# Layer-norm beta by accumulating transfers, gamma on VectorE and rstd on ScalarE or VectorE, and the last w2 tile pair by plain products, in an eight-core encoder kernel

## The chip, the cores and the metric

The kernel runs on all eight cores of one Trainium2 chip (two dies of four cores), one sequence of the batch on each core, without traffic between cores. The metric is the device time of the slowest core in microseconds (us).

A program on all eight cores has two states on this chip. In the slow one, the cores of one die or of both are granted a lower TensorE clock and take some per cent longer. Each run therefore carries a state, and only fast runs enter a verdict. I also give the **undisturbed cores**: over all runs of a kernel, the median span of the cores whose granted clock was within 0.012 of the ninth decile of that kernel's clocks. It leaves out the wait for the slowest core, so it is some 5 to 10 us below a fast run's time, but it is steady. I compare it only with the kernel before on the same chip.

## The reference

Two post-norm layers over x of shape (8, 2048, 1024) in float32. Each layer is a token mixer and a dense MLP, and each of these is followed by a layer norm, so there are four norms:

```python
x = layer_norm(alpha * x + mix, ln_g[i, 0], ln_b[i, 0])
x = layer_norm(alpha * x + squared_relu_mlp(x, mlp_w1[i], mlp_w2[i]), ln_g[i, 1], ln_b[i, 1])

def layer_norm(x, g, b):          # cut
    y = (xf - mu) * lax.rsqrt(var + LN_EPS) * g + b
```

Mixer 0 is a gated MLP with 128-position blocks, mixer 1 a short gated convolution. The MLP has 4096 hidden units. beta (`b` above, `ln_b`) is one row of 1024 numbers for each norm, the same for all positions.

## The kernel before

A Python scheduler lays out all operations. Each operation states what it reads and writes and for how long it is thought to run; a list scheduler gives each engine its order, and semaphores are added for the dependences. Each engine runs its own queue in order. A paced transfer gets a wait for the oldest transfers still out until no more than 1.6 MB are out:

```python
DMA_WINDOW = 1.6e6
DMA_RATE = 290e3                  # bytes per us that the model takes for every transfer
...
if op.is_dma:
    while op.paced and low < len(issued) and total - issued[low][0] > DMA_WINDOW:
        op.deps.setdefault(issued[low][1].idx, True)     # wait for that transfer's landing
        low += 1
    issued.append((total, op))
    total += op.nbytes
```

The sequence is worked in two halves (`h`) of 1024 positions, eight tiles of 128 (`tt`). The weights come in float32 from memory (HBM), are cast to f16 by the transfer, and are issued from GpSimd (POOL). Most products of the MLP are one-level Strassen: seven products in place of eight for a pair of tiles, with VectorE (DVE) building the sums and differences in f16 (`sub16`, line 405 in the profiles).

After each of the three inner norms the f16 copy for the next products is made at once, and the float32 residual is finished later ("deferred"), by two passes on VectorE:

```python
def scaled(tt, s, lnc):           # z = (z - mean) * gamma, then z * rstd + beta
    add("dve", ... scalar_tensor_tensor(out=z, in0=z, scalar=s.buf[:, 24:25], in1=lnc.buf[:, 0, :], op0=ALU.add, op1=ALU.mult), lazy=True)
    add("dve", ... scalar_tensor_tensor(out=z, in0=z, scalar=s.buf[:, 26:27], in1=lnc.buf[:, 1, :], op0=ALU.mult, op1=ALU.add), lazy=True)
```

The final norm (`final_tile`) normalises on ScalarE (ACT) in two halves of 512, and its gamma and beta passes go to POOL or VectorE, as the scheduler finds room; SyncE (SP) stores the tile:

```python
add("act", ... activation(out=z, in_=z, func=AF.Identity, scale=rstd, bias=nb))
scale = lambda e: e.tensor_tensor(z, z, lnc.buf[:, 0, sl], op=ALU.mult)
add("dve", None, ..., lazy=True, either={"pool": (scale, 1.3), "dve": (scale, t_dve(512))})
shift = lambda e: e.tensor_tensor(o.buf[:, sl], z, lnc.buf[:, 1, sl], op=ALU.add)
add("dve", None, ..., lazy=True, either={"pool": (shift, 1.3), "dve": (shift, t_dve(512))})
add("sp", ... dma_start(out=out_ap[r0:r0 + 128, :], in_=o.buf[:, 0:D]), paced=False)
```

Only the very last tile does it in two VectorE passes. The staging buffers `o` come from a pool of six ("sc"), from which the Strassen differences of the next tile pair are taken too.

## Time and profile before

| kernel before | |
|---|---|
| time, first six runs | 1528.93 us median (1500.81 to 1594.99) |
| profiled run | 1526.85 us |
| TensorE busy | 96% of the span |
| undisturbed cores of that run | 1485 to 1500 us |

The page of the slowest core (core 4), its first lines and the two DMA queues (q0 holds the transfers issued from POOL, q1 those from SP; the last number is the time of their packets as a share of the 16 DMA engines' span):

```profile
span 1525.3 us, 24043 instructions; the slowest of 8 cores (1485.3 to 1525.3 us)
...
PE 1456.9 (96%) x7300; PEld 688.7 (45%) x7300; DVE 1066.3 (70%) x2040; ACT 707.2 (46%) x1263; POOL 297.6 (20%) x464
...
q0 software_dynamic: 46656, 112.74, 48.1%
q1 hardware_dynamic: 7944, 27.37, 6.7%
```

The cores of the same run. Cores 4 and 5 had the lower clock; core 6 is undisturbed, and I read the kernel before from it:

```profile
core 4: 1525.3 us, clock 0.964
...
core 6: 1485.3 us, clock 0.986
...
die 0 (median of its cores): 1491.8 us, clock 0.984
```

What TensorE (PE) of core 6 waited for; the columns are total, number of times and longest wait in us. No wait is over 3.2 us:

```profile
PE ps L448 <- DVE xres L716: 6.9, 6, 2.9
PE ps L595 <- DVE xb L735: 6.4, 6, 2.0
PE ps L448 <- DVE wq L405: 6.3, 2, 3.2
...
PE ps L448 <- DVE sc L405: 5.0, 2, 2.5
```

Where PE is idle inside the program: windows of core 6, busy us of each engine with the number of its instructions, then the granted clock, the share of the DMA engines and GB/s. Up to about 700 us PE works on the second w1 stage of the last MLP; the final norm of the first half runs from about 700 to 750 us, and again from about 1450 us to the end at 1485 us:

```profile
675.00:700.00 25.00, 24.97 (x125) 11.55 (x124) 22.26 (x41) 13.76 (x25) 3.94 (x8) 1.00 0.61 105
700.00:725.00 25.00, 22.20 (x123) 10.77 (x121) 23.23 (x50) 10.67 (x20) 9.43 (x12) 1.00 0.61 121
725.00:750.00 25.00, 19.73 (x105) 9.25 (x106) 22.92 (x33) 13.06 (x23) 17.87 (x17) 1.00 0.78 175
1450.00:1473.00 23.00, 18.25 (x82) 7.51 (x80) 17.34 (x37) 9.62 (x16) 15.53 (x11) 1.00 0.28 113
```

The order of the engines in these lines is PE, PEld, DVE, ACT, POOL. In 725 to 750 us PE is busy 19.7 of 25 us, while DVE is at 92% and POOL at 71%. The groups on VectorE in 695 to 750 us say why (the last figure before the waits is the mean ns of one instruction):

```profile
L405 DVE TENSOR_TENSOR sc<-H,sc 128x1024 f16<-128x1024 f16 x4 | 9.2, 2298 | 0.0
L405 DVE TENSOR_TENSOR sc<-H 128x1024 f16<-128x1024 f16 x6 | 8.2, 1396 | 0.4 <-issue 0.4
L405 DVE TENSOR_TENSOR sc<-sc,H 128x1024 f16<-128x1024 f16 x4 | 2.7, 682 | 0.0
```

The first of these groups in 1320 to 1345 us, where POOL does nothing:

```profile
L405 DVE TENSOR_TENSOR sc<-H,sc 128x1024 f16<-128x1024 f16 x4 | 2.7, 684 | 0.0
```

Of the fourteen differences eleven took 0.68 us, and three took 5.6, 5.0 and 2.2 us. Each of the three had POOL's gamma or beta passes beside it, and ended some 0.55 us after the last of these. The longest one and the POOL passes beside it, from the timeline (start us, us, what):

```profile
714.28 5.58 DVE L405 TENSOR_TENSOR sc<-H,sc 128x1024 f16<-128x1024 f16 x1
714.36 2.50 POOL L672 TENSOR_TENSOR xres<-xres,lnc 128x512 f32<-128x512 f32 x2
716.83 2.48 POOL L675 TENSOR_TENSOR sc<-xres,lnc 128x512 f32<-128x512 f32 x2
```

Four POOL passes in a row held up one difference. The differences together lost about 10.7 us. That is the waste that the change is after.

### The profile page before, as it was taken

What the parts mean: (1) busy time and instruction counts of PE and PEld (TensorE: products, weight loads), DVE (VectorE), ACT (ScalarE), POOL (GpSimd) and SP (SyncE); (2) the same over time, 40 slices, a digit from 0 to 9 for tenths busy, and PEclk for the clock granted to TensorE, in tenths of its full rate; (3) what the DMA queues carried; (4) which work ended last, traced back from release to release, by engine and by line L of the source; (5) the groups of instructions that cost most, each with busy time, mean ns of one, the idle gap of its engine ahead of it and who ended that gap; (6) DMA issues with size and microseconds to landing.
All of it is one profiled execution on the core that took longest, in us unless ns stands there. A gap on an engine that the chain in (4) does not pass through costs nothing.

```text
span 1525.3 us, 24043 instructions; the slowest of 8 cores (1485.3 to 1525.3 us)
## 1 busy us (share of the span) xinstructions
PE 1456.9 (96%) x7300; PEld 688.7 (45%) x7300; DVE 1066.3 (70%) x2040; ACT 707.2 (46%) x1263; POOL 297.6 (20%) x464
## 2 busy tenths in 40 slices
PE   7999998999999989999989999899999999899995
PEld 3444454444464444444444444444444644444442
DVE  3246787848886777747872667877588857887787
ACT  2346655226562475025464565651356525740543
POOL 1124222011001111011351232210110111010116
PEclk8999999999999998888999999999999999999998
DMA  8997039277327754096589920581971467444702
GB/s 181 137 135 125 1 57 150 44 119 108 51 44 110 110 85 75 7 143 100 111 213 169 145 42 1 88 137 25 146 114 19 60 101 125 69 63 73 121 1 111
DMA packets 54727, 141.66 MB, mean 93 GB/s; under 512 B 6328, under 2 KB 6328, under 8 KB 54600
## 3 DMA queue, kind: packets, MB, share of 16 engines
q0 software_dynamic: 46656, 112.74, 48.1%
q1 hardware_dynamic: 7944, 27.37, 6.7%
q8 instruction: 62, 1.02, 0.3%
q14 instruction: 65, 0.53, 0.1%
HBM read 244.42 MB, written 8.39 MB: 166 GB/s over the span
## 4 chain that ended last, share of the span: by engine, by line
PE 73%; DMA 17%; issue 4%; DVE 3%; ACT 2%; POOL 1%; DVEq 0%; SPq 0%; POOLq 0%; ACTq 0%
PE ps L448 44%; PE ps L434 15%; DMA wq<-wbig 13%; PE ps L570 11%; DMA ws<-wsm 2%; PE ps L595 1%; ACT xT L611 1%; DMA sc<-rows 1%; DMA xres<-x 1%; DVE sc L405 1%; PE ps L898 0%; DVE xres L719 0%; PE ps L573 0%; DMA lnc<-rows 0%; ACT sc L633 0%
## 5 line engine op out<-in xcount | busy, mean ns | idle before, releaser
L434 PE MATMUL ps<-xT,ws 128*128 128x512 f16 (+1 forms) x1808 | 347.5, 354 | 1.0 <-DVE xT L605 0.9
L448 PE MATMUL ps<-wq,sc 128*128 128x512 f16 x1024 | 241.9, 389 | 12.2 <-DVE xres L716 6.2
L434 PEld LDWEIGHTS ps<-xT,ws 128*128 128x128 f16 x1808 | 179.6, 100 | 162.6 <-issue 10.8
L392 POOL DMA_DIRECT2D ws<-wsm x208 | 111.1, 534 | 572.7 <-PE ps L434 214.0
L719 DVE SCALAR_TENSOR_TENSOR xres<-xres,ps 128x512 f32<-128x512 f32 x192 | 131.4, 685 | 96.6 <-PE ps L448 73.2
L448 PE MATMUL ps<-wq,H 128*128 128x512 f16 x768 | 183.2, 387 | 1.1 <-ACT ps L401 1.1
L448 PE MATMUL ps<-xT,ws 128*128 128x512 f16 x672 | 173.4, 392 | 2.9 <-DMA ws<-wsm 2.1
L570 PE MATMUL ps<-wq,H 128*128 128x512 f16 x768 | 170.0, 379 | 2.3 <-DMA wq<-wbig 2.3
L448 PEld LDWEIGHTS ps<-wq,sc 128*128 128x128 f16 x1024 | 101.1, 100 | 139.9 <-issue 39.3
L392 POOL DMA_DIRECT2D wq<-wbig x104 | 55.8, 537 | 418.1 <-PE ps L448 202.8
L401 ACT ACTIVATE ps<-ps 128x512 f32<-128x512 f32 x88 | 51.5, 586 | 176.5 <-PE ps L448 164.2
L448 PE MATMUL ps<-wq,wt 128*128 128x512 f16 x448 | 121.6, 399 | 8.9 <-DVE wq L405 6.3
L570 PE MATMUL ps<-wq,xT 128*128 128x512 f16 x512 | 121.5, 380 | 4.3 <-DMA wq<-wbig 3.2
L448 PEld LDWEIGHTS ps<-wq,H 128*128 128x128 f16 x768 | 76.0, 99 | 94.0 <-issue 17.9
L570 PEld LDWEIGHTS ps<-wq,H 128*128 128x128 f16 x768 | 74.5, 98 | 92.1 <-issue 4.0
L611 ACT ACTIVATE xT<-ps,gbT_sb 128x256 f16<-128x256 f32 (+1 forms) x240 | 102.2, 535 | 17.4 <-PE ps L595 17.4
L448 PEld LDWEIGHTS ps<-xT,ws 128*128 128x128 f16 x672 | 65.4, 100 | 91.6 <-issue 38.0
L633 ACT ACTIVATE xb<-xres,st 128x1024 bf16<-128x1024 f32 x48 | 55.1, 1159 | 82.7 <-DVE st L630 82.4
L405 DVE TENSOR_TENSOR wq<-wq 128x2048 f16<-128x2048 f16 x64 | 78.0, 1219 | 4.6 <-DMA wq<-wbig 4.4
L570 PEld LDWEIGHTS ps<-wq,xT 128*128 128x128 f16 x512 | 49.3, 98 | 63.0 <-issue 6.4
L448 PEld LDWEIGHTS ps<-wq,wt 128*128 128x128 f16 x448 | 44.8, 101 | 66.5 <-issue 29.0
L867 DVE BATCH_NORM_STATS2 st<-sc 128x6 f32<-128x512 f16 x64 | 42.4, 686 | 42.1 <-ACT sc L865 42.1
(156 smaller groups left out, 1878.1 us busy)
## 6 DMA issues: line engine op xcount, KB each, us to landing
ws<-wsm POOLq DMA_DIRECT2D x208, 256.0 KB, 5.3
wq<-wbig POOLq DMA_DIRECT2D x104, 512.0 KB, 7.0
lnc<-rows SPq DMA_DIRECT2D x20, 512.0 KB, 10.2
xres<-x SPq DMA_DIRECT2D x16, 512.0 KB, 6.6
out<-sc SPq DMA_DIRECT2D x15, 512.0 KB, 3.3
xb<-x POOLq DMA_DIRECT2D x8, 256.0 KB, 5.1
sc<-rows POOLq DMA_DIRECT2D x2, 512.0 KB, 9.3
wt<-wsT POOLq DMA_DIRECT2D x2, 256.0 KB, 6.6
```

The costliest lines, as they stand in the source:

```text
L392: add("pool", lambda e: e.dma_start(out=dst(), in_=src), writes=w, dma=stream, nbytes=nbytes, dur=0.55)
L401: add("act", lambda e: e.activation(out=dst.buf[:], in_=src.buf[:], func=AF.Copy), reads=[src], writes=w, dur=t_act(512))
L405: add("dve", lambda e: e.tensor_tensor(out(), a(), b(), op=op), reads=reads, writes=writes, dur=t_dve(n, True))
L434: ins = e.matmul(bk.buf[:, p * n * 128:(p + 1) * n * 128], ws.buf[:, kc, :], xT[:, kc, t0 * 128:(t0 + n) * 128], start=(kc == 0 and not be ...
L448: ins = e.matmul(bk.buf[:], lhs(kc), rhs(kc), start=(first and kc == 0), stop=(kc == nk - 1), skip_group_check=True)
L570: ins = e.matmul(bk.buf[:], A[:, kc, tt * 128:(tt + 1) * 128], wqs[kc // 4].buf[:, kc % 4, :], start=(kc == 0), stop=(kc == nk - 1 and bia ...
L595: ins = e.matmul(bk.buf[:, o:o + 128], xb.buf.bitcast(FH)[:, c * 128:(c + 1) * 128], ident[:], start=(o == 0), stop=(o == 384), skip_group ...
L611: ins = e.activation(out=out[:, j], in_=src()[:, j], func=AF.Identity, scale=gbT[:, gb, c:c + 1], bias=gbT[:, 4 + gb, c:c + 1])
L633: add("act", lambda e: e.activation(out=junk.buf.bitcast(mybir.dt.bfloat16)[:, 0:D], in_=z, func=AF.Square, bias=s.buf[:, 24:25], accum_ou ...
L719: add("dve", lambda e: e.scalar_tensor_tensor(out=xres[:, tt, sl], in0=xres[:, tt, sl], scalar=ALPHA if alpha else 1.0, in1=bk.buf[:], op0 ...
L867: add("dve", lambda e, a=a, b=b, cb=cb: e.bn_stats(s.buf[:, 6 * cb:6 * cb + 6], v16(a, b)), reads=[(vn, cb)], writes=[(s, cb)], dur=0.69)
```

## The change

The intent is to take beta off the compute engines and POOL's passes out of the final norm.

- **Inner norms** (48 tiles): one VectorE pass for mean and gamma, an rstd pass on ScalarE or VectorE, and beta added by an accumulating transfer of 512 KB from HBM onto the residual in SBUF.
- **Final norm** (16 tiles): the output in HBM is first filled with beta, one 4 MB transfer for each half, HBM to HBM; the tiles are then added to it by accumulating stores.
- The deferred work moves from the first w2 stage into the w1 groups (`catch_up`), the norm's constants become two buffers of half the size, and a marker (`f_begun`) keeps the first w2 product behind the last w1 copy.
- The **last tile pair** of all uses plain products (64 in place of 56), so that tile 6 ends before tile 7.

```diff
-        P.pool("lnc", [sb(f"lnc{i}", [128, 2, D], F32) for i in range(1)])
+        P.pool("lnc", [sb(f"lnc{i}", [128, D], F32) for i in range(2)])
...
+        def gain(tt, s, lnc, out, wr, sl, lazy):            # z = (z - mean) * gamma; out = z * rstd
+            add("dve", lambda e: e.scalar_tensor_tensor(out=z, in0=z, scalar=s.buf[:, 24:25], in1=lnc.buf[:, sl],
+                                                        op0=ALU.add, op1=ALU.mult), ...)
+            add("act", None, ..., either={"act": (activation Copy, scale=rstd), "dve": (tensor_scalar mult rstd)})
...
-        def scaled(tt, s, lnc):                             # two VectorE passes
+        def scaled(tt, s, lnc, idx):
+            gain(tt, s, lnc, lambda: z, both, slice(0, D), True)
+            add("pool", lambda e: e.dma_start(out=z, in_=row_bc((4 + idx) * 1024, 1024), accum_op=ALU.add),
+                writes=both, dma=("ac", tt), nbytes=128 * 8192, dur=0.55)
+
+        def shift_out(h, dep):
+            r0 = h * NT * 128
+            add("sp", lambda e: e.dma_start(out=out_ap[r0:r0 + 1024, :], in_=row_bc(7 * 1024, 1024, 1024)),
+                reads=[dep], writes=[("out", h)], dma=("ob", h), nbytes=1024 * 4096, dur=0.06)
...
         def final_tile(h, tt, s, lnc):                      # ACT, POOL/DVE passes and plain store go
+            for a in (0, 512) if last else (0,):
+                gain(tt, s, lnc, lambda sl=sl: o.buf[:, sl], wr, sl, not last)
+                add("pool", lambda e, sl=sl: e.dma_start(out=out_ap[r0:r0 + 128, sl], in_=o.buf[:, sl], accum_op=ALU.add),
+                    reads=wr + [("out", h)], ..., dur=0.55, paced=False)
...
                 if fh == 1:
                     lnc = load_lnc(l * 2 + 1)
+                    if final:
+                        shift_out(h, w2["22"][1])           # once the last w2 block has landed
...
+                    if end and t0 == NT - 2:                # last pair: plain products
+                        for tt in (t0, t0 + 1):
+                            for cb, ks in enumerate((("11", "21"), ("12", "22"))):
+                                residual(tt, cb, gemm_T(tt, w2[ks[0]] + w2[ks[1]]), False, s)
+                            final_tile(h, tt, s, lnc)
+                        break
```

Cuts are marked with "...", and some calls are shortened.

More of the change, by code (lines that the diff above doesn't have):

```diff
@@ L415, in load_lnc @@
             v = vt("lnc")
-            for j, r in ((0, idx), (1, 4 + idx)):
-                add("sp", lambda e, j=j, r=r: e.dma_start(out=v.buf[:, j, :], in_=row_bc(r * 1024, 1024)),
-                    writes=[(v, j)], dma=("lnc", j), nbytes=128 * 4096, dur=0.06)
+            add("sp", lambda e: e.dma_start(out=v.buf[:], in_=row_bc(idx * 1024, 1024)), writes=[v], dma=v,
+                nbytes=128 * 4096, dur=0.06)
             return v
@@ L492, in strassen_F @@
             prod(a, W(w0, 0), X(0, 0), True)
-            copy_psum(b, a, [b])
+            copy_psum(b, a, [b, "f_begun"])
             prod(f, TW(1), SX(1), True)
@@ L533, in prod @@
                 product(bk, x[0], w[0], 8, first, w[1] + x[1])
-            prod(a, A(t0, 0), B("11"), True)
+            product(a, A(t0, 0)[0], B("11")[0], 8, True, A(t0, 0)[1] + B("11")[1] + ["f_begun"])
             copy_psum(b, a, [b])
@@ L547, in strassen_T, with strassen_wq @@
             residual(t1, 0, f, False, sums[1])
-        def strassen_wq(blk):
+        def strassen_wq(blk, keep=False):
             w = {}
@@ L552, in strassen_wq @@
                 q = [load_wq(blk + cb, i) for i in range(4)]
-                w["11" if cb == 0 else "T1"], w["21" if cb == 0 else "22"] = q[:2], q[2:]
-            for n in ("T3", "T2", "T4"):
-                w[n] = [vt("wq"), vt("wq")]
+                w["11" if cb == 0 else "12"], w["21" if cb == 0 else "22"] = q[:2], q[2:]
+            for n in ("T3", "T1", "T2", "T4"):
+                w[n] = w["12"] if n == "T1" and not keep else [vt("wq"), vt("wq")]
             flat = lambda v: (lambda: v.buf[:].rearrange("p a b -> p (a b)"))
-            for o, x, y in (("T3", "22", "T1"), ("T1", "T1", "11"), ("T2", "22", "T1"), ("T4", "21", "T2")):
+            for o, x, y in (("T3", "22", "12"), ("T1", "12", "11"), ("T2", "22", "T1"), ("T4", "21", "T2")):
                 for i in range(2):
@@ L637, in row_stats @@
             rstd(s, lambda: s.buf[:, 25:26], 1.0 / D, pool)
-        def scaled(tt, s, lnc):
-            z, both = xres[:, tt, :], [(("xres", tt), 0), (("xres", tt), 1)]
-            add("dve", lambda e: e.scalar_tensor_tensor(out=z, in0=z, scalar=s.buf[:, 24:25], in1=lnc.buf[:, 0, :],
-                                                        op0=ALU.add, op1=ALU.mult),
-                reads=both + [(s, "nm"), (lnc, 0)], writes=both, dur=t_dve(1024), lazy=True)
-            add("dve", lambda e: e.scalar_tensor_tensor(out=z, in0=z, scalar=s.buf[:, 26:27],
-                                                        in1=lnc.buf[:, 1, :], op0=ALU.mult, op1=ALU.add),
-                reads=both + [(s, "rs"), (lnc, 1)], writes=both, dur=t_dve(1024), lazy=True)
+        def gain(tt, s, lnc, out, wr, sl, lazy):
+            z, n = xres[:, tt, sl], sl.stop - sl.start
+            ks = [(("xres", tt), q) for q in range(2) if sl.start <= q * 512 < sl.stop]
+            add("dve", lambda e: e.scalar_tensor_tensor(out=z, in0=z, scalar=s.buf[:, 24:25], in1=lnc.buf[:, sl],
+                                                        op0=ALU.add, op1=ALU.mult),
+                reads=ks + [(s, "nm"), lnc], writes=ks, dur=t_dve(n), lazy=lazy)
+            add("act", None, reads=ks + [(s, "rs")], writes=wr, lazy=lazy, either={
+                "act": (lambda e: e.activation(out=out(), in_=z, func=AF.Copy, scale=s.buf[:, 26:27]), t_act(n, True) + 0.1),
+                "dve": (lambda e: e.tensor_scalar(out(), z, s.buf[:, 26:27], None, op0=ALU.mult), 0.08 + n * 0.00055)})
+        def scaled(tt, s, lnc, idx):
+            z, both = xres[:, tt, :], [(("xres", tt), 0), (("xres", tt), 1)]
+            gain(tt, s, lnc, lambda: z, both, slice(0, D), True)
[5 more added lines that the diff above has]
+                reads=[dep], writes=[("out", h)], dma=("ob", h), nbytes=1024 * 4096, dur=0.06)
         def final_tile(h, tt, s, lnc):
@@ L652, in final_tile @@
             r0 = (h * NT + tt) * 128
-            if not last:
-                add("dve", lambda e: e.tensor_tensor(s.buf[:, 2:3], s.buf[:, 24:25], s.buf[:, 26:27], op=ALU.mult),
-                    reads=[(s, "nm"), (s, "rs")], writes=[(s, "nb")], dur=0.16)
-            for q in range(2):
-                sl = slice(q * 512, (q + 1) * 512)
-                k = (("xres", tt), q)
-                z = xres[:, tt, sl]
-                if last:
-                    add("dve", lambda e, z=z, sl=sl: e.scalar_tensor_tensor(
-                        out=z, in0=z, scalar=s.buf[:, 24:25], in1=lnc.buf[:, 0, sl], op0=ALU.add, op1=ALU.mult),
-                        reads=[k, (s, "nm"), (lnc, 0)], writes=[k], dur=t_dve(512))
-                    add("dve", lambda e, z=z, sl=sl: e.scalar_tensor_tensor(
-                        out=o.buf[:, sl], in0=z, scalar=s.buf[:, 26:27], in1=lnc.buf[:, 1, sl],
-                        op0=ALU.mult, op1=ALU.add),
-                        reads=[k, (s, "rs"), (lnc, 1)], writes=[(o, q)], dur=t_dve(512))
-                else:
-                    add("act", lambda e, z=z: e.activation(out=z, in_=z, func=AF.Identity, scale=s.buf[:, 26:27],
-                                                           bias=s.buf[:, 2:3]),
-                        reads=[k, (s, "nb"), (s, "rs")], writes=[k], dur=t_act(512, True) + 0.1)
-                    scale = lambda e, z=z, sl=sl: e.tensor_tensor(z, z, lnc.buf[:, 0, sl], op=ALU.mult)
-                    add("dve", None, reads=[k, (lnc, 0)], writes=[k], lazy=True,
-                        either={"pool": (scale, 1.3), "dve": (scale, t_dve(512))})
-                    shift = lambda e, z=z, sl=sl: e.tensor_tensor(o.buf[:, sl], z, lnc.buf[:, 1, sl], op=ALU.add)
-                    add("dve", None, reads=[k, (lnc, 1)], writes=[(o, q)], lazy=True,
-                        either={"pool": (shift, 1.3), "dve": (shift, t_dve(512))})
-                if last:
-                    add("sp", lambda e, sl=sl: e.dma_start(out=out_ap[r0:r0 + 128, sl], in_=o.buf[:, sl]),
-                        reads=[(o, q)], dma=o if q else ("sc", "last"), nbytes=128 * 2048, dur=0.06, paced=False)
@@ L681, in final_tile @@
-            if not last:
-                add("sp", lambda e: e.dma_start(out=out_ap[r0:r0 + 128, :], in_=o.buf[:, 0:D]),
-                    reads=[(o, 0), (o, 1)], dma=o, nbytes=128 * 4096, dur=0.06, paced=False)
-        def normed(tt, s, lnc, pool):
+            for a in (0, 512) if last else (0,):
+                sl = slice(a, a + (512 if last else D))
+                wr = [(o, q) for q in range(2) if sl.start <= q * 512 < sl.stop]
+                gain(tt, s, lnc, lambda sl=sl: o.buf[:, sl], wr, sl, not last)
+                add("pool", lambda e, sl=sl: e.dma_start(out=out_ap[r0:r0 + 128, sl], in_=o.buf[:, sl], accum_op=ALU.add),
+                    reads=wr + [("out", h)], dma=o if sl.stop == D else ("sc", "last"), nbytes=128 * 4 * (sl.stop - sl.start),
+                    dur=0.55, paced=False)
@@ L686, in normed @@
+        def normed(tt, s, lnc, pool, idx):
             z, zk = xres[:, tt, :], ("xres", tt)
@@ L697, in normed @@
                                                              s.buf[:, 26:27], op0=ALU.add, op1=ALU.mult), 0.54)})
-            deferred.append(lambda: scaled(tt, s, lnc))
+            deferred.append(lambda: scaled(tt, s, lnc, idx))
             return xb
@@ L703, in layer_norm_tile @@
         def layer_norm_tile(tt, s, idx, lnc, pool, S=None):
-            pending.append(normed(tt, s, lnc, pool))
+            pending.append(normed(tt, s, lnc, pool, idx))
             if len(pending) == 2 or tt >= NT - 2:
@@ L793, in init_gate @@
             dma_cast(lambda: vg.buf.bitcast(FH)[:, 0:2048], row_bc(12 * 1024, 2048), [vg], ("c4", gc.seq), 128 * 8192)
-            bs = vt("lnc")
-            add("sp", lambda e: e.dma_start(out=bs.buf[:, 1, :], in_=row_bc(11 * 1024, 1024)), writes=[(bs, 1)],
-                dma=("lnc", 1), nbytes=128 * 4096, dur=0.06)
+            bs = load_lnc(11)
             for r in range(2):
@@ L804, in init_gate @@
                         scalar=cols[:, 32 + 8 * r + i:33 + 8 * r + i],
-                        in1=bs.buf[:, 1, (4 * r + i // 2) * 128:(4 * r + i // 2 + 1) * 128],
+                        in1=bs.buf[:, (4 * r + i // 2) * 128:(4 * r + i // 2 + 1) * 128],
                         op0=ALU.mult, op1=ALU.add),
-                        reads=[bk, "cols", (bs, 1)], writes=[(bias2[r], 8 * r + i)], dur=0.28)
+                        reads=[bk, "cols", bs], writes=[(bias2[r], 8 * r + i)], dur=0.28)
             return wsT, vg, bias2
         def add_bout():
-            bo = vt("lnc")
-            add("sp", lambda e: e.dma_start(out=bo.buf[:, 0, :], in_=row_bc(8 * 1024, 1024)), writes=[(bo, 0)],
-                dma=("lnc", 0), nbytes=128 * 4096, dur=0.06)
+            bo = load_lnc(8)
             for tt in range(NT):
@@ L816, in add_bout @@
                 add("dve", lambda e, tt=tt: e.scalar_tensor_tensor(
-                    out=xres[:, tt, :], in0=xres[:, tt, :], scalar=ALPHA, in1=bo.buf[:, 0, :],
+                    out=xres[:, tt, :], in0=xres[:, tt, :], scalar=ALPHA, in1=bo.buf[:],
                     op0=ALU.mult, op1=ALU.add),
-                    reads=both + [(bo, 0)], writes=both, dur=t_dve(1024))
+                    reads=both + [bo], writes=both, dur=t_dve(1024))
         def gate_mixer(h, gc):
@@ L995, in square @@
                             reads=[t], writes=[("H", fc, tb * 4 + i) for i in range(4)], dur=t_dve(512, True))
+                    catch_up()
                     if g < ng:
@@ L1012, in mlp @@
                     strassen_F(cur, S, square)
-                w2 = strassen_wq(BIG_BASE[f"w2_{l}"] + fh * 2)
+                end = h == 1 and final and fh == 1
+                w2 = strassen_wq(BIG_BASE[f"w2_{l}"] + fh * 2, end)
                 if fh == 1:
                     lnc = load_lnc(l * 2 + 1)
+                    if final:
+                        shift_out(h, w2["22"][1])
                 nxt = prep_T(0)
                 for t0 in range(0, NT, 2):
+                    if end and t0 == NT - 2:
+                        for tt in (t0, t0 + 1):
+                            s = vt("st")
+                            for cb, ks in enumerate((("11", "21"), ("12", "22"))):
+                                residual(tt, cb, gemm_T(tt, w2[ks[0]] + w2[ks[1]]), False, s)
+                            final_tile(h, tt, s, lnc)
+                        break
                     cur = nxt
-                    if t0 + 2 < NT:
+                    if t0 + 2 < NT and not (end and t0 == NT - 4):
                         nxt = prep_T(t0 + 2)
-                    catch_up()
-                    catch_up()
                     sums = [vt("st"), vt("st")] if fh == 1 else [None, None]
```

## The prediction

> **What bounds the kernel now.** TensorE: the page gives PE 96% of the span, the chain of waits 73% PE. The cores table shows that the clock makes the spread (1485 to 1525 us at 0.987 to 0.964). On core 6 (1485.3 us, undisturbed) the waits view names only about 40 us of PE idle: the start, layer-norm boundaries with transposes (untouched by the change), and the two final-norm stages. In the windows 700-725 and 725-750 PE is busy 22.2 and 19.7 of 25 us; in 1450-1473, 18.3 of 23 us; from the start of the last product to the end there are 12.7 us. The change can reach these places only, some 25 us.
>
> **Why PE waits there.** The windows show DVE 92% and POOL 71% busy in 725-750. The groups in 695-750 give the f16 differences for the next tile pair 1396 and 2298 ns, against 684 ns in 1320-1345 where POOL is idle: ten of them lost about 10.6 us to POOL's gamma/beta passes (1.26 us each). The Trainium skill, "SBUF — State Buffer", section "Who interferes with whom", says that a VectorE instruction with two SBUF inputs contends with a GpSimd instruction that reads SBUF; the trace agrees by these numbers.
>
> **What the change does.**
> - Final norm: removes POOL's passes (39 x about 1.35 us; 21 more are on DVE) and two ACT passes of 0.8 us per tile; adds one DVE pass of 1.28 us and an rstd pass on ACT (estimate 1.15-1.25 us, from 1.15 for the square of that size) or DVE (estimate 0.7 us). DVE's work is nearly even, but uncontended: 6 of 8 us of PE idle back in 700-750 and 4 of 4.7 us in 1450-1473.
> - The 48 inner norms: one of two 1.28 us DVE passes becomes an ACT or DVE pass plus an accumulating transfer: 30-50 us of DVE work, off the critical path (PE is 99-100% busy there): about 0 us.
> - This deferred work moves from the first w2 stage into w1, where DVE had some 4.7 us of work per 6 us of PE and comes about even with it: loss 0-3 us.
> - Last pair: 64 products for 56, +1.7 us; but tile 6 ends early and the tail has no POOL pass. The tail before is 12.3 us after the last product; after, I estimate 8.5-10. Net of both -1 to -2 us.
> - Transfers: 48 accumulations of 512 KB, two 4 MB fills of the output, 17 accumulating stores. A 512 KB load or store alone takes 1.4 us of all engines; at two to three times that, the 55% DMA share rises by about 10 points. The w1 windows have 49-64%, so PE should not feel it. The Trainium skill, "DMA: Bandwidth & Descriptors", section "SWDGE vs HWDGE vs iDMA", says accumulation must be issued from GpSimd: these transfers now queue in order with the weight loads, a possible loss of 0-4 us. No run shows yet what one costs.
>
> Sum: -10 -1.5 +3, about -9 to -11 us with rounding, 0.7%.
>
> **Predicted time** 1518 us, range 1492 to 1545, mostly for the clock's spread. Faster by over 2%: 0.07; within 2%: 0.85; slower by over 2%: 0.08.
>
> **Right if:** in the final stages POOL's tensor passes are gone, the f16 differences are near 690 ns, PE is over 95% busy; DVE busy falls 30-60 us; DMA share is up about 10 points; the tail shrinks by 2-4 us.
>
> **Wrong if:** weight loads land late because the POOL queue stood behind accumulations or the fill; PE waits in w1 on DVE; the fill delays the output accumulations and holds their buffers; the accumulating store lands so slowly that the tail grows; or a denser PE is granted a lower clock.

## The result

The changed kernel is slower: 1555.47 us median of 10 runs (1550.89 to 1687.36), against 1522.17 us median of 20 runs of the kernel before. The ratio of the fast runs is 1.0353, 95% interval 1.0308 to 1.0398. (A ratio is the mean time of one kernel's fast runs over that of the other's fast runs of the same rounds, so it is not quite the ratio of the medians.) It gives the right result.

The page of the slowest core (core 6):

```profile
span 1552.2 us, 24067 instructions; the slowest of 8 cores (1539.9 to 1552.2 us)
...
PE 1438.2 (93%) x7308; PEld 681.6 (44%) x7308; DVE 1011.8 (65%) x2003; ACT 717.2 (46%) x1260; POOL 301.5 (19%) x489
...
q0 software_dynamic: 56016, 146.30, 58.7%
q1 hardware_dynamic: 6424, 23.18, 6.8%
```

VectorE has 54 us less work, as wanted, and TensorE was busy a smaller share of a longer span. All cores are alike, with a lower mean clock than before:

```profile
core 6: 1552.2 us, clock 0.970
...
die 1 (median of its cores): 1548.9 us, clock 0.972
```

What TensorE waited for on this core. The first line is new, and alone about as long as the whole loss, some 50 us on undisturbed cores (1546 us, against 1494 to 1501 us for the kernel before on the chips of the experiments):

```profile
PE ps L447 <- DVE wt L405: 49.4, 4, 23.5
PE ps L569 <- DMA wq<-wbig: 6.6, 4, 3.9
```

"DVE wt L405" builds the Strassen differences of w1, and it was not slow itself. The chain of work that ended last, from 655 to 712 us, in order (start us, us, what):

```profile
653.32 8.58 DMA wq<-wbig
661.97 40.72 DMA out<-rows
...
703.37 3.90 DMA ws<-wsm
...
707.37 0.44 DVE wt L405
...
707.94 4.42 PE ps L447 x10
```

One goes back from the product at 707.94 us: it waited for differences, these for a w1 block (`ws`), and the load of that block was issued only when the fill of the output (`out<-rows`) had landed, 40.7 us after its issue. The POOL queue in these us (the bracket is the idle time before, and what ended it):

```profile
659.49 0.53 POOL L392 DMA_DIRECT2D ws<-wsm  x1 [0.19 <-issue]
703.37 2.26 POOL L392 DMA_DIRECT2D ws<-wsm  x4 [43.35 <-DMA out<-rows]
```

For 43 us not one weight was asked for. The windows of this core, for those shown of before (same columns):

```profile
675.00:700.00 25.00, 8.99 (x53) 4.18 (x50) 9.56 (x18) 6.29 (x11) 0.00 (x0) 0.80 0.99 120
700.00:725.00 25.00, 15.04 (x52) 5.31 (x53) 9.36 (x21) 5.37 (x10) 6.36 (x12) 0.73 0.84 130
725.00:750.00 25.00, 24.89 (x122) 11.54 (x122) 19.26 (x41) 8.21 (x15) 4.24 (x8) 1.00 0.76 121
750.00:775.00 25.00, 24.73 (x134) 11.83 (x132) 17.00 (x42) 11.54 (x21) 3.93 (x6) 1.00 0.56 109
1450.00:1475.00 25.00, 5.60 (x14) 2.06 (x15) 3.65 (x9) 0.82 (x2) 2.65 (x5) 0.52 0.51 133
```

In 675 to 700 us PE is idle for 16 us while the DMA engines are at 99%. It happens again in the second half, at 1450 to 1475 us. The clock column explains the lower mean clock: it is 0.80, 0.73 and 0.52 in the windows with the long waits, 1.00 in the others. (1.00 - 0.80 + 1.00 - 0.73 + 1.00 - 0.52) x 25 us is about 24 us, or 1.5% of the span, and 0.985 to 0.970 is just that. The Trainium skill, "TensorE: Matmul & The Clock Gate", Part 1, says that TensorE falls to half clock after some 3.4 us of idleness and needs as long at work to come back; this agrees, with 0.52 over a window that is mostly one wait. So the low clock follows from the waits and is not another cause.

The final norm itself became what was hoped for. The groups on VectorE in 740 to 790 us:

```profile
L641 DVE SCALAR_TENSOR_TENSOR xres<-xres,st,lnc 128x1024 f32<-128x1024 f32 x8 | 10.1, 1276 | 0.1
L405 DVE TENSOR_TENSOR sc<-H 128x1024 f16<-128x1024 f16 x4 | 2.7, 688 | 4.7 <-DMA out<-sc 3.7 <-PE ps L447 0.9
L405 DVE TENSOR_TENSOR sc<-H,sc 128x1024 f16<-128x1024 f16 x3 | 2.1, 687 | 0.0
```

The f16 differences are back from means of 1396 and 2298 ns to under 690 ns, and PE is busy 24.7 of 25 us in 750 to 775 us. But a new wait stands in the second line: 3.7 us for a store of the output, whose buffer the differences need.

The transfers (size, and median us from issue to landing):

```profile
xres<-rows POOLq DMA_DIRECT2D x48, 512.0 KB, 6.1
...
out<-rows SPq DMA_DIRECT2D x2, 4096.0 KB, 41.0
out<-sc POOLq DMA_DIRECT2D x15, 512.0 KB, 10.0
```

Before, the stores took 3.3 us to land:

```profile
out<-sc SPq DMA_DIRECT2D x15, 512.0 KB, 3.3
```

### The profile page after: what moved, and what is told of

Its sections match the earlier page's. It is cut to its first block, busy times and chain, and to the rows that moved or that the text cites. A ratio compares the mean times of both kernels' runs of the same rounds, so it can differ in the third digit from the quotient of the medians.

```text
span 1552.2 us, 24067 instructions; the slowest of 8 cores (1539.9 to 1552.2 us)
## 1 busy us (share of the span) xinstructions
PE 1438.2 (93%) x7308; PEld 681.6 (44%) x7308; DVE 1011.8 (65%) x2003; ACT 717.2 (46%) x1260; POOL 301.5 (19%) x489
## 3 DMA queue, kind: packets, MB, share of 16 engines
q0 software_dynamic: 56016, 146.30, 58.7%
q1 hardware_dynamic: 6424, 23.18, 6.8%
## 4 chain that ended last, share of the span: by engine, by line
PE 67%; DMA 22%; issue 4%; ACT 3%; DVE 3%; POOL 0%; POOLq 0%; DVEq 0%; SPq 0%; ACTq 0%
PE ps L447 37%; PE ps L433 14%; PE ps L569 13%; DMA wq<-wbig 9%; DMA out<-rows 5%; DMA ws<-wsm 4%; PE ps L594 2%; ACT xT L610 1%; DMA out<-sc 1%; DMA xres<-x 1%; DVE wq L405 1%; DMA sc<-rows 1%; PE ps L881 1%; ACT xb L632 0%; DMA xres<-rows 0%
## 5 line engine op out<-in xcount | busy, mean ns | idle before, releaser
L433 PE MATMUL ps<-xT,ws 128*128 128x512 f16 (+1 forms) x1808 | 340.3, 348 | 3.9 <-DMA ws<-wsm 1.1
L433 PEld LDWEIGHTS ps<-xT,ws 128*128 128x128 f16 x1808 | 176.2, 98 | 161.0 <-issue 9.4
L447 PE MATMUL ps<-wq,sc 128*128 128x512 f16 x992 | 228.4, 383 | 6.1 <-DVE wq L405 4.5
L569 PE MATMUL ps<-wq,H 128*128 128x512 f16 x832 | 188.1, 384 | 6.5 <-DMA wq<-wbig 5.0
L447 PE MATMUL ps<-xT,ws 128*128 128x512 f16 x672 | 168.8, 382 | 5.6 <-ACT xT L610 2.0
L447 PE MATMUL ps<-wq,H 128*128 128x512 f16 x744 | 171.8, 379 | 0.1
L447 PEld LDWEIGHTS ps<-wq,sc 128*128 128x128 f16 x992 | 97.1, 99 | 126.1 <-issue 13.7
L569 PEld LDWEIGHTS ps<-wq,H 128*128 128x128 f16 x832 | 81.8, 99 | 106.7 <-issue 13.4
L447 PEld LDWEIGHTS ps<-wq,H 128*128 128x128 f16 x744 | 72.4, 98 | 86.4 <-issue 0.3
L610 ACT ACTIVATE xT<-ps,gbT_sb 128x256 f16<-128x256 f32 (+1 forms) x240 | 102.2, 540 | 13.8 <-PE ps L594 13.3
L447 PEld LDWEIGHTS ps<-xT,ws 128*128 128x128 f16 x672 | 63.7, 98 | 91.3 <-issue 22.6
L651 POOL DMA_DIRECT2D xres<-rows x48 | 43.0, 899 | 245.4 <-DVE xres L646 130.2
L641 DVE SCALAR_TENSOR_TENSOR xres<-xres,st,lnc 128x1024 f32<-128x1024 f32 (+1 forms) x65 | 84.3, 1303 | 3.0 <-ACT sc L632 1.5
L405 DVE TENSOR_TENSOR wt<-ws 128x512 f16<-128x512 f16 x112 | 46.6, 419 | 50.3 <-DMA ws<-wsm 48.5
```

The costliest lines, as they stand in the source:

```text
L405: add("dve", lambda e: e.tensor_tensor(out(), a(), b(), op=op), reads=reads, writes=writes, dur=t_dve(n, True))
L433: ins = e.matmul(bk.buf[:, p * n * 128:(p + 1) * n * 128], ws.buf[:, kc, :], xT[:, kc, t0 * 128:(t0 + n) * 128], start=(kc == 0 and not be ...
L447: ins = e.matmul(bk.buf[:], lhs(kc), rhs(kc), start=(first and kc == 0), stop=(kc == nk - 1), skip_group_check=True)
L569: ins = e.matmul(bk.buf[:], A[:, kc, tt * 128:(tt + 1) * 128], wqs[kc // 4].buf[:, kc % 4, :], start=(kc == 0), stop=(kc == nk - 1 and bia ...
L610: ins = e.activation(out=out[:, j], in_=src()[:, j], func=AF.Identity, scale=gbT[:, gb, c:c + 1], bias=gbT[:, 4 + gb, c:c + 1])
L641: add("dve", lambda e: e.scalar_tensor_tensor(out=z, in0=z, scalar=s.buf[:, 24:25], in1=lnc.buf[:, sl], op0=ALU.add, op1=ALU.mult), reads= ...
```

## The experiments

Two theories at first. **A**: the wait is the cost; the fill counts 4 MB against a window of 1.6 MB, so the next weight load is made to wait for its landing. **B**: the traffic is the cost; the fill keeps the DMA engines busy for 40 us, and any weight load beside it would crawl. A rival to both, **C**: it is the accumulating transfers on the POOL queue.

All edits below are to the changed kernel if not said otherwise. Every edit makes the scheduler lay out the whole program anew, so differences of 2 or 3 us mean little. In the diffs of this part calls are shortened. e1 to e4 ran on one chip, and one of its dies was slow in all runs: none of the four has a ratio, so what was expected of ratios could not be tested, and I read the undisturbed cores.

### e1: the fill outside the window

```diff
-                issued.append((total, op))
-                total += op.nbytes
+                if not (isinstance(op.stream, tuple) and op.stream[0] == "ob"):
+                    issued.append((total, op))
+                    total += op.nbytes
```

> The changed kernel with one edit: the 4 MB fill is not counted in the 1.6 MB window of outstanding transfers, so no weight load is made to wait for its landing; it still runs at the same time. Theory A (the wait that the window makes is the cost): the 22 to 24 us PE waits near 684 and 1447 us shrink below 4 us each, ratio to before about 0.99 to 1.01. Theory B (the fill takes the engines or the memory from the weight loads, the wait is incidental): waits of 10 us or more stay, ratio 1.02 to 1.04. Theory C (the loss lies in the accumulating transfers on the POOL queue, not in the fill): ratio stays near 1.035.

Measured: right result. Undisturbed cores 1530.2 us, before 1500.8 us: 29 us slower, where the whole change is some 50 us slower. The long waits break into many short ones. TensorE's waits on core 6:

```profile
PE ps L448 <- DVE wt L406: 19.8, 7, 4.4
PE ps L448 <- DMA ws<-wsm: 10.1, 3, 6.1
```

The fill now needs 51.0 us to land (core 6). Weight loads issued beside the first fill landed up to 36 us after their issue, where the median of the whole run is 5.6 us, and POOL waited up to 14.1 us at once for one. No wait of TensorE reaches the 10 us of theory B, but two kinds are over the 4 us of theory A. Neither theory is right alone: without the wait some 20 us come back, and some 30 us stay with the traffic.

### e2: the fill alone, in the kernel before

Edit: `shift_out` as in the change is added to the kernel before, and its plain stores wait for the fill and overwrite it.

> The kernel before, with the two 4 MB fills of the output alone added at the same place; its plain stores wait for the fill and overwrite it, so the result is right. Theories A and B: the fill alone brings the whole loss, two PE waits of 20 us or more in the second w1 stage of the last layer, ratio 1.03 to 1.045. Theory C: ratio under 1.01.

Measured: right result, undisturbed cores 1521.8 us, before 1500.8 us: 21 us slower. Theory C is out as the main cause: the fill costs without a single accumulating transfer. But my expectation for A and B missed: it brings less than half of the loss, and not at the expected place. It was scheduled later here (687 us), and the load that came late was that of x for the next half (15.3 us of waiting at once). What a blocked queue costs depends on what stands behind it.

### e3: the final norm and stores as before

Edit: `final_tile` of before in place of that of the change, and no fill; the inner accumulations, the moved catch-up and the plain last pair stay.

> The changed kernel with the final norm and its plain stores as before, no fill and no accumulating store; the 48 inner accumulations, the moved catch-up and the plain last pair stay. Theories A and B: no PE wait over 4 us in w1, ratio 0.995 to 1.005 (the POOL passes of the final norm are back, so their 8 us are too). Theory C: ratio 1.02 or more.

Measured: right result, undisturbed cores 1494.1 us, before 1500.8 us: 7 us faster. No wait of TensorE over 2.3 us in w1. Everything in the change but its final norm is harmless or a small gain, which rules out C for the inner accumulations.

### e4: the fill in eight pieces

```diff
-            add("sp", ... dma_start(out=out_ap[r0:r0 + 1024, :], in_=row_bc(7 * 1024, 1024, 1024)), ...)   # once
+            add("sp", ... dma_start(out=out_ap[r0:r0 + 128, :], in_=row_bc(7 * 1024, 1024)), ...)          # after each w1 group
```

> The changed kernel with each fill cut in eight transfers of 512 KB, one after each group of the second w1 stage, all in the window. Theory A: no weight load waits long, PE waits under 4 us, ratio 0.985 to 1.00. Theory B (the traffic itself, 37 us of it in a stage of some 50 us, starves the loads): PE waits in w1 of 10 us and more in sum, ratio over 1.01.

Measured: right result, undisturbed cores 1513.8 us, before 1500.8 us: 13 us slower. The waits in w1 are gone, as A has it. But each piece takes 11.4 us to land (median, core 6), the loads of x for the next half come late (one wait of 9.6 us), and the loss of 0.9% is close to B's line. Spreading the same traffic moved the wait from w1 to the change of halves.

### e5, e6, e12: how the fill is made

So the question became why 4 MB take 40 us, when a store of 512 KB alone takes 1.4 us. Three fills at the same place. e5: from a beta tile in SBUF, in eight stores of 512 KB.

```diff
-            add("sp", ... dma_start(out=out_ap[r0:r0 + 1024, :], in_=row_bc(7 * 1024, 1024, 1024)), ...)
+            b = load_lnc(7)
+            for tt in range(NT):
+                add("sp", ... dma_start(out=out_ap[r0:r0 + 128, :], in_=b.buf[:]), ..., nbytes=128 * 4096)
```

> The changed kernel with the fill sent from a beta tile in SBUF: at the same place, in eight stores of 512 KB, all in the window. Theory D (the fill is costly because memory to memory it moves only about 100 GB/s and keeps all 16 engines busy for some 40 us; the window's wait only decides what stands behind it): the eight stores take 10 to 18 us in all, PE waits in the second w1 stage under 5 us each, undisturbed cores within 10 us of the kernel before, either side. Theory A (the wait alone, any 4 MB in the window does it): with the window full of 512 KB pieces the waits are short as well, so A is not told apart here, but A gives no reason for the time of the stores. Theory E (4 MB of writes to memory are slow whatever the source): the stores take 30 us or more and PE waits of 10 us or more stay.

e6: from HBM as in the change, but from 1024 different rows (`in_=x_ap[r0:r0 + 1024, :]`), with a wrong result.

> The changed kernel with the fill read from 1024 distinct rows of x instead of 1024 times the one beta row; wrong result on purpose. If one row read over and over is what makes the fill slow, it lands in 20 us or less and the PE waits shrink by half or more; if memory to memory is slow in itself, it lands in 35 to 45 us and the two waits of 22 us stay.

e12: from the SBUF tile, but as one 4 MB transfer, so that the window treats it like the fill of the change.

> The changed kernel with the fill from SBUF as one 4 MB transfer, which the window treats as the fill of the change (everything after it waits for its landing). If the time of the transfer is what counts and the window only passes it on, it lands in 12 to 18 us, PE waits in w1 stay under 5 us each and undisturbed cores are within 5 us of the kernel with eight pieces (about equal to before). If a 4 MB entry in the window is costly in itself, PE waits of 8 us or more show in w1 and it is 10 us or more slower than that.

The transfer lines of e6 and of e12, each from the profile's list of transfers:

```profile
out<-x SPq DMA_DIRECT2D x2, 26.7
```

```profile
out<-lnc SPq DMA_DIRECT2D x2, 4096.0 KB, 16.1
```

| fill | lands in us | counted as one 4 MB entry | undisturbed cores, us against before |
|---|---|---|---|
| HBM, one row (the change) | 41.0 | yes | about +50 |
| HBM, one row, outside the window (e1) | 51.0 | no | +29 |
| HBM, 1024 rows, larger packets (e6, one run) | 26.7 | yes | +22 |
| SBUF, one transfer (e12) | 16.1 | yes | +8 |
| SBUF, eight pieces (e5) | 6.5 each | no | -1 |

For e5 the ratio of fast runs is 0.997 (0.983 to 1.011), for e12 0.992 (0.988 to 0.997). For e12 both fast runs of the kernel before were at its upper level (1523 and 1524 us), so I rely on the undisturbed cores there. The eight stores of e5 took 25 to 28 us from the first issue to the last landing (cores 1 and 2), more than the 10 to 18 us expected: their issue was itself spread over some 20 us.

What follows: the slow transfer and the wait both count, and the wait costs more when the transfer is slow. With the transfer from SBUF the entry in the window costs some 9 us (e12 against e5); with the transfer from HBM it costs some 20 us (the change against e1). The source is the root: 41 us from one row of HBM, 27 us from x in HBM, 16 us from SBUF. My expectation for e6 had only "20 us or less" and "35 us or more", and the landing fell between; the two long waits of TensorE in w1 were 10.9 and 9.5 us (core 4), about half of those of the change. That e12 was expected within 5 us of e5 was wrong as well; it was 9 us.

So a copy from memory to memory is slow even from x. Why it is slower still from one row is not shown, because e6 changed two things. Its page has fewer packets in q1 than that of the change (6424):

```profile
q1 hardware_dynamic: 4504, 23.18, 6.4%
```

In the trace of e6 each fill went in 64 packets of 64 KB, in that of the change in 1024 packets of 4 KB. No run read distinct rows in packets of 4 KB, so either the repeated row or the small packets may be what costs 14 us more. Small packets alone do not make a fill slow: the fill of e12 from SBUF went in packets of 4 KB as well.

What limits the copy inside the memory stays open. It is not the engines' occupancy alone: on core 6 the packets of the first fill took 35.5 us of all 16 engines' time and those of the second 14.1 us, and both fills took about 37 us from the first packet to the last.

### e7, e13, e14: where the expected gain went

e7: no fill at all, the accumulating stores kept; wrong result.

> The changed kernel without the fill, the accumulating stores kept; wrong result on purpose (it adds to whatever the output holds). Theories A and D: no PE wait over 5 us in w1; undisturbed cores 5 to 12 us faster than before (the POOL passes are gone). If the accumulating stores cost something themselves (10 us to landing, on the POOL queue), it is within 4 us of before or slower.

Measured: undisturbed cores 1490.7 us, before 1494.4 us: only 4 us faster. Ratio of fast runs 0.992 (0.980 to 1.004), so unclear. The four fast runs are at 1498 to 1502 us, against 1502 to 1524 us. So the fill explains the loss (some 50 us over before with it, 4 us under without it), but the gain of 9 to 11 us that I had predicted for the rest is not there. Two more runs without fill and without beta. Their outputs are wrong, which doesn't matter for the times. e13 takes the accumulation away and leaves the stores on POOL:

```diff
-                add("pool", ... dma_start(out=out_ap[r0:r0 + 128, sl], in_=o.buf[:, sl], accum_op=ALU.add), ...)
+                add("pool", ... dma_start(out=out_ap[r0:r0 + 128, sl], in_=o.buf[:, sl]), ...)
```

> The changed kernel without the fill, its final stores plain instead of accumulating but still issued from POOL; wrong result on purpose (no beta in the output). If the accumulation's slow landing is what costs (stores land in about 10 us and hold the buffers of the next differences), the stores land in 3 to 5 us, the tail after the last product is 3 us or more shorter and undisturbed cores are 8 us or more faster than the kernel without fill (1491 us). If the place on the POOL queue costs, it is within 3 us of that.

e14 issues them from SP as well.

> The same with the plain stores issued from SyncE; wrong result on purpose. If the POOL queue costs, this is 5 us or more faster than the run before it; if the accumulation costs, within 2 us of it, and both within 4 us of the version with two VectorE passes (1474 us); if the rstd pass on ScalarE costs, both stay 8 us or more slower than that.

Stores of e7 and of e13, from the list of transfers of each:

```profile
out<-sc POOLq DMA_DIRECT2D x15, 512.0 KB, 9.1
out<-sc POOLq DMA_DIRECT2D x2, 256.0 KB, 7.5
```

```profile
out<-sc POOLq DMA_DIRECT2D x15, 512.0 KB, 5.1
out<-sc POOLq DMA_DIRECT2D x2, 256.0 KB, 2.5
```

| stores (no fill) | land in us (512 KB, 256 KB) | from the start of the last product to the end | undisturbed cores against before |
|---|---|---|---|
| accumulating, POOL (e7) | 9.1, 7.5 | 14.4 to 15.8 us | 1490.7, -4 |
| plain, POOL (e13) | 5.1, 2.5 | 9.5 to 9.8 us | 1476.0, -18 |
| plain, SP (e14) | 3.6, 2.1 | 8.2 to 8.6 us | 1474.2, -20 |

(The third column is from the eight cores of each profile; for the kernel before it is 12.7 us, for the changed kernel 14.1 to 15.6 us.) The accumulation alone costs 14 us. About 5 us of it stand at the end, where the last two stores land 5 us later. Where the other 9 us go is shown only in part. On core 2 the stores hold their buffers longer: in e7 VectorE's differences waited 4.0 us for a store once and POOL's loads of x 7.1 us, in e13 2.0 and 0.8 us. On core 6 the same waits are 2.6 and 1.0 us, against 2.2 and 1.0 us, so this is not the whole account. The POOL queue as such costs about 2 us, no more than a new layout may move, and the rstd pass on ScalarE nothing that shows (e14 ends within 1 us of e8 below).

### e8 and e15: the final norm in two VectorE passes

No fill, no accumulating store, nothing on POOL: every final tile as the last one was in the kernel before, with plain stores from SP. The result is right.

```diff
+                add("dve", ... scalar_tensor_tensor(out=z, in0=z, scalar=mean, in1=gamma, op0=ALU.add, op1=ALU.mult), lazy=not last)
+                add("dve", ... scalar_tensor_tensor(out=o.buf[:, sl], in0=z, scalar=rstd, in1=beta, op0=ALU.mult, op1=ALU.add), lazy=not last)
+                add("sp", ... dma_start(out=out_ap[r0:r0 + 128, sl], in_=o.buf[:, sl]), paced=False)
```

> No fill and no accumulating store: the final norm in two VectorE passes of 1.28 us (gamma, then rstd and beta), plain stores from SyncE, nothing on POOL; the inner accumulations and the plain last pair stay. If POOL's passes are what holds PE in the final stage, its f16 differences take about 690 ns, PE idle in the final stage falls to 2 us or less in each half, tail about 10 us; undisturbed cores 8 to 15 us faster than before. If VectorE's load is what counts, PE idle stays at 5 us or more per half and the gain is under 5 us.

> The version with the final norm in two VectorE passes and plain stores once more, unchanged: undisturbed cores 15 to 22 us faster than the kernel before, ratio of fast runs 0.985 to 0.99.

Measured: undisturbed cores 1474.4 us (before 1494.4 us), and in e15 1475.8 us (before 1493.9 us): 20 and 18 us faster (8 to 15 us were expected for e8, 15 to 22 us for e15). e8's fast runs are 1481 us once and 1497 and 1498 us with one pair of cores at a lower clock; the ratio of 0.986 (0.972 to 1.000) is unclear, and e15 (fast runs 1503 and 1520 us) has no ratio. So the gain is read from the undisturbed cores alone; in the time of the slowest core, which is the metric, it is not shown. In e15 no run was under 1500.9 us, where the kernel before had 1501.2 and 1502.9 us in the same rounds: in every run of e15 some cores had a lower clock. The time of e8 to the end after the last product starts was expected at about 10 us and is 13.8 us. The final stage of the first half on core 2 of e8:

```profile
695.00:745.00 50.00, 49.45 (x268) 23.90 (x267) 40.10 (x83) 18.44 (x37) 6.87 (x13) 1.00 0.68 131
```

PE is busy 49.5 of 50 us, and VectorE at 80% with work that nothing disturbs. This is the version that I would keep: its fastest run is 1481 us, where the kernel before never went under 1499.9 us and the changed one never under 1550.9 us, and it is simpler than the change.

### e9, e10, e11: the parts of that version

> The kernel before with one edit: its final norm in two VectorE passes (gamma, then rstd and beta), nothing on POOL or ACT, plain stores. The version with this, the inner accumulations and the plain last pair was about 19 us faster on undisturbed cores. If the POOL passes of the final norm are most of what could be won, this alone gives 10 to 16 us on undisturbed cores; if the rest of the change brings most, under 6 us.

> The version with the final norm in two VectorE passes, but the 48 inner norms with two VectorE passes as before instead of accumulating transfers (moved catch-up and plain last pair stay). If the inner accumulations are off the critical path, as predicted, within 3 us of the version with them (about 17 to 21 us under before on undisturbed cores); if the VectorE time saved in w1 counts, 5 us or more slower than it; if the accumulations in the POOL queue hold weight loads, 3 us or more faster.

> The version with the final norm in two VectorE passes, with the last pair of tiles in seven products again. The prediction put the plain pair at 1 to 2 us gained in net: then this is 1 to 2 us slower than that version; over 4 us slower if the tail gains more than estimated; faster if the eight more products cost more than the tail gives.

All three on one chip (before 1494.8 us on undisturbed cores), right results:

| kernel | undisturbed cores | against before | start of the last product to the end |
|---|---|---|---|
| e9: before, final norm in two VectorE passes | 1478.1 | -17 | 16.2 us |
| e10: e8 without the inner accumulations | 1478.9 | -16 | 13.9 us |
| e11: e8 without the plain last pair | 1481.4 | -13 | 19.5 us |
| e8, e15 (other chips) | 1474.4, 1475.8 | -20, -18 | 13.8 us |

Of the three, e10 has a ratio of 0.989 (0.985 to 0.993), and e11 one of 0.980 (0.965 to 0.995), which is unclear; in both the fast runs of the kernel before were those at 1523 and 1524 us, as for e12. e9 has one fast run (1487 us) and no ratio.

The one edit to the final norm (e9) brings nearly all of the gain, a little above what I expected. The inner accumulations are worth 2 to 4 us (e10 against e8 and e15), which agrees with "about 0" within what a new layout may move. The plain pair is worth 5 to 7 us in this version (e11 against e8), more than expected, and all of it at the end of the program (19.5 against 13.8 us). These parts do not add up to the whole.

## Why the prediction was wrong

- **What was right.** TensorE is the bound. POOL's passes stretched VectorE's differences, and these went back to 687 ns. In 750 to 775 us PE is busy 24.7 of 25 us. VectorE's busy time fell by 54 us (30 to 60 predicted). q0's DMA share rose from 48.1 to 58.7% (about 10 points predicted). The w1 stages did not become VectorE-bound, and the inner accumulations are off the critical path (e3, e10).
- **The step that failed**, as the prediction put it: "A 512 KB load or store alone takes 1.4 us of all engines; at two to three times that, the 55% DMA share rises by about 10 points. The w1 windows have 49-64%, so PE should not feel it", and "these transfers now queue in order with the weight loads, a possible loss of 0-4 us". The fill was only counted as bytes. By that price 4 MB are 11 us, or 22 to 34 us of the engines' time at two to three times it; the first fill of core 6 took 35.5 us of it, and the DMA share rose as predicted. So the bytes were not priced far off. What was wrong is "so PE should not feel it": the fill took 41 us to land, and nothing in the sum asked what waits for its landing. It was in none of the queues that I watched: it is issued from SP, but the pacing rule, which stood in the code before me, ties every later weight load on POOL to its landing. The term put at 0 to 4 us measured about 50 us: roughly 20 for the wait and 30 for the traffic (e1), and about 3 for a fill from SBUF in pieces (e5 against e7). "Wrong if" named "the POOL queue stood behind accumulations or the fill" as a risk, without a size.
- **The second step**: the tail, "after, I estimate 8.5-10" us against 12.3 us. On core 6 it is 14.9 us from the end of the last product (2.6 us more), because an accumulating store of 256 KB takes 7.8 us to land there (7.5 us in e7, against 2.5 us for a plain one in e13). With plain stores from SP the tail is a little shorter than estimated: 8.2 us even from the start of the last product (e14).
- **The gain of 9 to 11 us** for the rest came out at 4 us (e7), as the slow accumulating stores took back 14 us (e13). What plain arithmetic on VectorE could win there was larger than I thought: 17 us (e9).
- **The clock** was no cause: the lower mean is the warm-up after two long waits.

## What to carry to other kernels

Price a transfer by its kind, not by its bytes: source, destination and accumulation changed the time to landing of the same bytes by factors of 1.8 to 3 here. Then look at what a late landing would hold up, which is every queue that a pacing rule or a semaphore ties to it, not only the queue it is issued from. And before work is moved off a compute engine, ask whether that engine was short of time or merely disturbed: with POOL silent, VectorE had room for both passes, and the simplest version did best on undisturbed cores. And look behind a mean: here three held-up instructions out of fourteen made it.

## What the Trainium skill lacked or had wrong

- "DMA: Bandwidth & Descriptors" has rates for loads from HBM to SBUF, and for copies between HBM tensors only at row pitches of 512 KiB and more; it has none for a fill like this one, whose rows lie 4 KB apart. Here 4 MB took 41 us on eight cores at once (about 102 GB/s for each core), and 16 us from SBUF to HBM. "HBM Reference", Specifications, gives about 358 GB/s per core; an estimate from that page, 8 MB read and written, is 23 us, a little over half of what was measured.
- "DMA: Bandwidth & Descriptors", "Rules for kernel authors", allows a repeated source ("A source may repeat (a broadcast)") and tells of a cost only for fewer than 16 copies in the outermost dimension. From one row of 4 KB a 4 MB copy took 41 us, in packets of 4 KB; from 1024 different rows it took 27 us, in packets of 64 KB, and no run parts the two. Loads of one row to the 128 partitions of SBUF were faster: two of 512 KB with nothing beside them took 3.7 us from the first packet to the last in the kernel before.
- The same page, "SDMA does more than copy", names accumulation without a price. An accumulating store of 512 KB from POOL landed in 9.1 us and a plain one in 5.1 us; 256 KB in 7.5 and 2.5 us. The 65 accumulating transfers added about 204 us of all 16 engines' time on the POOL queue of core 6 (58.7% of 1552 us less 47.6% of 1485 us), some 3 us each, against 1.3 us for a plain store of 512 KB with nothing beside it.
- "SBUF — State Buffer", "Who interferes with whom", was right that the two contend, and has no size for these instructions: of fourteen f16 differences eleven took 0.68 us, and three took 5.6, 5.0 and 2.2 us, each until some 0.55 us after the last POOL pass beside it.
